# Dividing the softmax weights ahead of their transposes, and multiplying by the values with the values stationary

## The chip, the cores and the metric

The kernel runs on one core of a Trainium2 chip. Its engines work side by side: TensorE (PE in the profile, its weight loads as PEld), VectorE (DVE), ScalarE (ACT), GpSimd (POOL) and SyncE (SP, which issues most of the DMAs). Each engine runs its instructions in a fixed order and waits where an instruction needs something that another engine has not finished. The metric is the time of one execution on the device in microseconds (us): before the change the median of three runs is 1180.84 us (1177.32 to 1181.2).

## What is computed

A small network on 256 tokens with 1024 features, in fp32: a first block with mixers, attention to a memory and a feed forward, and then a second block with two layers. The change is in the attention of these two layers. Each layer has 16 heads of 64 features:

```python
# 4 latent heads ("mla"), 8 dilated heads, 4 heads on selected keys ("dsa"); for each head:
s = q @ k.T * scale
s = where(mask, s, -inf)              # causal; by distance; or causal and among the 64 best keys
p = softmax(s, axis=-1)               # = exp(s - max) / sum
o = p @ v                             # (256 queries, 64 features)
x = x + concat(o of all heads) @ w_o  # then the feed forward
```

## The kernel before

Activations lie feature by feature, 128 features on the partitions and 256 tokens along the row. Weights stream from HBM in chunks; ACT rounds a chunk to `whi` (L409), DVE takes the rest `wlo` (L410), and a product of an activation with a weight is three fp32r matmuls, L428 to L430 (activations are split likewise, by `split`, L457: a copy on ACT, L460, and a difference on DVE, L461). The matmuls of the attention itself are plain fp32 (helper `mm`, L450), and in the trace each of them is two records with a weight load of its own; transposes on PE (helper `tr`, L454) are one record.

The heads go in pairs. The pairs of a layer are called M0 and M1 (latent), D0 to D3 (dilated), S0 and S1 (selected), and the list `ATTN` (L38) sets the order in which their steps are emitted between the projections: M0, M1, D0, D1, D3, D2, S0, S1. The framework's scheduler then orders the instructions of each engine; a projection's three matmuls stand between the steps of the pairs, so that PE has work while a pair's softmax runs.

For a pair, `scores` (L1622) does: the score products of both heads into PSUM, 128 queries by 128 keys and 128 by 256 keys (`pss`, L450); four DVE instructions that add the mask, scale and take the row minimum (L1635, tile `as`); four exponentials on ACT that also give the row sums (L1638, into `ast`); one reciprocal of the four columns of sums (L1640). The weights are not yet divided.

`values` (L1643) does: three transposes a head (`pst<-ident,as`, L454), a copy of each head's 128x384 to SBUF on ACT (`apT`, L1653), then six products with the transposed weights stationary and the values streaming, 64 columns each (`po`, queries on the partitions); one DVE instruction that multiplies by the reciprocals as it reads PSUM (`ao`, L1659); two more transposes (`psf`, L454) back to features on the partitions; and the split into `aoh` and `aol`, which the output projection (`psW`) reads.

Along the same stretch DVE runs the selection of the 64 best keys (`topk`) that S0 and S1 need, and the rotations of queries and keys. POOL has nothing to do there.

Of the kernel before, what the change touches and what calls it, by code (L numbers as in the profile page):

```python
# [16 lines left out]
P = 128  # L17
# [58 lines left out]
def _rot_cols(base, m):  # L76
    """two heads of 64 features, each pair of rotated ones 16 apart"""
    i = np.arange(P)
    return base + 64 * (2 * m + i // 64) + 16 * (i // 32 % 2) + i % 16 + 32 * (i // 16 % 2)
# [276 lines left out]
def weave(*gens):  # L356
    """emits the steps of several mixers in turn"""
    gens = list(gens)
    while gens:
        for g in list(gens):  # L360
            if next(g, gens) is gens:
                gens.remove(g)


class Net:
# [123 lines left out]
    def inv_root(self, pool, v, L, tag):  # L489
        """v: -1/2 of a positive value; L: the value's logarithm; returns the value ** -0.5"""  # L490
        nc = self.nc
        n = v.shape[1]
        y = pool.tile([P, n], F32, tag=tag, name="iy")
        self.xact(y, L, AF.Exp, scale=-0.5)
        t = self.tmp.tile([P, T], F32, tag="irt", name="irt")[:, :n]
        nc.vector.tensor_mul(t, y, y)
        nc.vector.tensor_mul(t, t, v)
        nc.vector.scalar_tensor_tensor(y, t, 1.5, y, ALU.add, ALU.mult)
        return y

    def mean(self, acc, tag):
        """-1/2 (mean + eps) on every partition, and the logarithm of mean + eps"""
# [10 lines left out]
    def cols(self, pool, rB):  # L513
        """[128, 256] the same on every partition -> a column for each token tile"""
# [7 lines left out]
    def sumsq(self, x, gains=(None,), accs=None, join=True, eng=None):  # L522
        """sums over the feature tiles of the squares, one for each gain"""
# [96 lines left out]
    def ffn(self, tag, g, fc, nt):  # L620
# [4 lines left out]
        with self.pool("ffn" + tag) as big, self.pool("fz" + tag, 3) as zp:  # L625
# [13 lines left out]
            # three steps, each two tiles behind the one before, so that no engine waits for another  # L639
# [60 lines left out]
    def block1_mix(self, es):  # L700
# [34 lines left out]
        # rotary tables  # L735
        ang = self.rope_angles(rs)

        # gated delta: q k v with the short convolution
# [111 lines left out]
    def delta(self, s, sm, gates):  # L850
        nc, m, b8, t2 = self.nc, self.mp, self.b8, self.t2
        # beta, log decay
# [17 lines left out]
        # l2 norms  # L870
# [28 lines left out]
        # value rows, scaled by beta  # L899
# [7 lines left out]
        # decay between tokens  # L907
# [20 lines left out]
        for b in range(3):  # L928
            pd = self.pb(512, "psd")
            t = b % 2 if b < 2 else 1  # L930
            # strict and its complement together sum over all tokens
# [23 lines left out]
        # inverse of the unit lower triangle, block doubling  # L955
# [12 lines left out]
        for k in range(1, 7):  # L968
            # only the left half of each pair of blocks changes
# [32 lines left out]
        # solve and read out  # L1002
# [18 lines left out]
    def read_out(self, i, Pm, v):  # L1021
        """Pm: weights [s, block, head, t]; v: [s, tile, head, 64]."""
# [43 lines left out]
    def log_sig(self, f, l):  # L1066
        """l <- ln(1 + exp(-|f|))"""
        nc = self.nc
        nc.scalar.activation(l, f, AF.Abs)
        self.xact(l, l, AF.Exp, scale=-1.0)  # L1070
        self.xact(l, l, AF.Ln, bias=self.one_c)

    def scan_levels(self, nf, lf, qb, k, name):
        """lf: log decay [t, tile, nf*128]; qb: [feat, nf, tile, heads, 128], zero outside its head;
        k: [feat, nf, tile, 128]; returns weights [s, block, head, t]."""
# [62 lines left out]
    def head_rows(self, dst, ps, nh, sc=None):  # L1138
        """dst: [feat, tile, head, 128], zero outside its head's rows; ps: [feat, 256]"""
# [11 lines left out]
    def hgrn(self, xh, xl, gates, tmaj):  # L1151
        nc, m, t2 = self.nc, self.mp, self.t2
        # lower bound
# [85 lines left out]
    def turns(self, xh, xl, cosR, sinR, wait, step):  # L1239
        """queries and keys of the retention, turned; a few products at a time"""  # L1240
# [141 lines left out]
    def block2(self):  # L1382
        from contextlib import ExitStack
        nc, x = self.nc, self.x
        # the first block's last norm and this block's first one
# [21 lines left out]
    def norm_pair(self, pool, s1, s2):  # L1407
        """the root of the first block's last norm, and of it with the next norm"""
# [13 lines left out]
    def attn(self, es, l, xh, xl):  # L1422
# [8 lines left out]
        # latents  # L1431
# [46 lines left out]
        # rotary tables with the norm folded in  # L1478
# [19 lines left out]
        # positions of the keys, scores of the index, queries from the latents  # L1498
# [123 lines left out]
    def scores(self, hs, mask, scale):  # L1622
        """hs: (q, k) of two heads; returns their weights, before the division, and the sums"""
# [16 lines left out]
        nc.vector.reciprocal(st[:, 1], st[:, 0])  # L1640
        return ws, st

    def values(self, ws, st, v, oh, ol, kt):  # L1643
        """v: the values of the two heads; writes feature tile kt of the output."""
        nc, pp = self.nc, self.pp
        po = self.pso.tile([P, 2, 2, 64], F32, tag="o", name="po")
        for i, s in enumerate(ws):
# [3 lines left out]
            # keys 0..127 for all queries, keys 128.. for the later ones  # L1651
            pT = self.p3.tile([P, 384], F32, tag="apT", name="apT")
            nc.scalar.copy(pT, pt)  # L1653
            vi = v[:, :, i * 64:(i + 1) * 64]
            self.mm(po[:, 0, i, :], pT[:, 0:P], vi[:, 0], start=i == 0)
            self.mm(po[:, 1, i, :], pT[:, P:T], vi[:, 0], start=False, stop=False)
            self.mm(po[:, 1, i, :], pT[:, T:384], vi[:, 1], start=False)
        o = pp.tile([P, 2, P], F32, tag="ao", name="ao")
        nc.vector.tensor_mul(o.rearrange("p t (h v) -> p t h v", h=2), po, st[:, 1].unsqueeze(3).to_broadcast([P, 2, 2, 64]))  # L1659
        pf = self.pb(T, "psf")  # L1660
        for t in range(2):
            self.tr(pf[:, t * P:(t + 1) * P], o[:, t])
        self.split(oh[:, kt, :], ol[:, kt, :], pf)
# [19 lines left out]
```

## Time and profile before

| | us |
|---|---|
| median of three runs (lowest, highest) | 1180.84 (1177.32, 1181.2) |
| span of the profiled execution | 1175.3 |
| lowest run less this span | 2.0 |
| median less this span | 5.5 |
| PE busy, share of the span | 1146.0 (98%) |
| DVE, ACT, POOL busy | 937.6 (80%), 668.4 (57%), 110.3 (9%) |
| chain that ended last: PE, DVE, ACT | 87%, 9%, 2% |

The span runs from the first to the last instruction on the core; a run's time has some microseconds around it. A busy PE is not a PE at its peak: matmuls are pipelined, and a record lasts longer than the distance to the next one. So costs on PE are read below from the starts of neighbouring records. The attention of the first of the two layers lies at about 562 to 640 us of the span, that of the second at about 887 to 966 us. The granted clock is full in nearly all slices.

### The profile page before, as it was taken

How to read it: one execution, taken by the hardware profiler on the slowest of the kernel's cores; microseconds unless marked ns; L12 is line 12 of the kernel's file. 1: busy time of each engine (PE TensorE's matmuls, PEld its weight loads, DVE VectorE, ACT ScalarE, POOL GpSimd, SP SyncE). 2: the span in 40 equal slices, each digit the busy share in tenths (PEclk: the TensorE clock that was granted, in tenths of full speed). 3: DMA queues.
4: the chain of work that ended last, by engine and by line, in shares of the span. 5: the costliest groups of instructions: out<-in, count | busy, mean ns of one | idle time of the engine just before them, and what ended most of it. 6: DMA issues, size and time to landing. Idle time of an engine off the chain costs nothing.

```text
span 1175.3 us, 23197 instructions
## 1 busy us (share of the span) xinstructions
PE 1146.0 (98%) x9148; PEld 1103.1 (94%) x9148; DVE 937.6 (80%) x1887; ACT 668.4 (57%) x1178; POOL 110.3 (9%) x137
## 2 busy tenths in 40 slices
PE   7999999999999999998999999999999999999996
PEld 7899888989999999997989999999988999999996
DVE  7987869587599997568897999985578978999854
ACT  6653545466576666554555766664545556766642
POOL 5500201010010000222000200001120002000000
PEclk9999999999999999998999999999999999999998
DMA  6522142556455656544324565555543235565652
GB/s 243 169 73 90 57 146 78 174 180 208 143 167 194 193 186 182 191 151 139 127 93 130 171 200 189 188 184 189 170 146 122 91 126 179 182 195 182 193 183 83
DMA packets 51948, 184.68 MB, mean 157 GB/s; under 512 B 5888, under 2 KB 6784, under 8 KB 51584
## 3 DMA queue, kind: packets, MB, share of 16 engines
q1 hardware_dynamic: 51408, 182.23, 47.9%
q8 instruction: 71, 1.16, 0.4%
q0 software_dynamic: 144, 0.46, 0.2%
q10 hardware_dynamic: 288, 0.52, 0.1%
q14 instruction: 37, 0.30, 0.1%
HBM read 182.14 MB, written 1.05 MB: 156 GB/s over the span
## 4 chain that ended last, share of the span: by engine, by line
PE 87%; DVE 9%; ACT 2%; issue 1%; DMA 1%; SPq 0%; POOL 0%; DVEq 0%; ACTq 0%
PE psU L430 10%; PE psU L429 10%; PE psU L428 10%; PE psD L430 5%; PE psD L428 5%; PE psD L429 5%; PE psp L428 3%; PE po L450 3%; PE psp L429 3%; PE psp L430 3%; PE psW L428 3%; PE psW L430 2%; PE psW L429 2%; DVE wlo L410 2%; PE pss L450 2%; PE pst L441 2%
## 5 line engine op out<-in xcount | busy, mean ns | idle before, releaser
L409 ACT ACTIVATE whi<-raw 128x1024 fp32r<-128x1024 f32 (+5 forms) x411 | 362.8, 898 | 316.6 <-PE psU L429 56.4
L410 DVE TENSOR_TENSOR wlo<-raw,whi 128x1024 fp32r<-128x1024 f32 (+5 forms) x411 | 423.3, 1041 | 140.7 <-ACT whi L409 139.5
L428 PE MATMUL psU<-xh,whi 128*128 128x256 f32 x1056 | 295.4, 280 | 0.0
L430 PE MATMUL psU<-xh,wlo 128*128 128x256 f32 x1056 | 294.9, 279 | 0.2 <-DVE wlo L410 0.2
L429 PE MATMUL psU<-xl,whi 128*128 128x256 f32 x1056 | 294.8, 279 | 0.0
L430 PEld LDWEIGHTS psU<-xh,wlo 128*128 128x128 f32 x1056 | 198.4, 188 | 0.4 <-DVE wlo L410 0.4
L429 PEld LDWEIGHTS psU<-xl,whi 128*128 128x128 f32 x1056 | 198.5, 188 | 0.1
L428 PEld LDWEIGHTS psU<-xh,whi 128*128 128x128 f32 x1056 | 198.5, 188 | 0.1
L428 PE MATMUL psD<-gh,whi 128*128 128x256 f32 x528 | 149.4, 283 | 0.0
L429 PE MATMUL psD<-gl,whi 128*128 128x256 f32 x528 | 149.4, 283 | 0.0
L430 PE MATMUL psD<-gh,wlo 128*128 128x256 f32 x528 | 149.4, 283 | 0.0
L533 POOL TENSOR_TENSOR ssa<-ssa,ssq 128x256 f32<-128x256 f32 x61 | 56.5, 931 | 722.7 <-ACT ssq L531 445.8
L664 DVE SCALAR_TENSOR_TENSOR y<-zb,prm,y 128x256 f32<-128x256 f32 x264 | 114.0, 478 | 0.0
L430 PEld LDWEIGHTS psD<-gh,wlo 128*128 128x128 f32 x528 | 101.4, 192 | 0.0
L429 PEld LDWEIGHTS psD<-gl,whi 128*128 128x128 f32 x528 | 101.3, 192 | 0.0
L428 PEld LDWEIGHTS psD<-gh,whi 128*128 128x128 f32 x528 | 101.3, 192 | 0.0
L428 PE MATMUL psp<-xh,whi 128*128 128x256 f32 (+1 forms) x288 | 85.3, 296 | 0.0
L429 PE MATMUL psp<-xl,whi 128*128 128x256 f32 (+1 forms) x288 | 84.0, 292 | 0.0
L430 PE MATMUL psp<-xh,wlo 128*128 128x256 f32 (+1 forms) x288 | 83.8, 291 | 0.0
L655 ACT ACTIVATE y<-zb,prm 128x256 f32<-128x256 f32 x132 | 67.2, 558 | 5.3 <-DVE zb L651 5.3
L428 PEld LDWEIGHTS psp<-xh,whi 128*128 128x128 f32 (+1 forms) x288 | 55.6, 193 | 3.1 <-issue 2.3
L429 PEld LDWEIGHTS psp<-xl,whi 128*128 128x128 f32 (+1 forms) x288 | 55.3, 192 | 1.1 <-issue 1.0
(456 smaller groups left out, 2342.6 us busy)
## 6 DMA issues: line engine op xcount, KB each, us to landing
raw<-in_wst_dram SPq DMA_DIRECT2D x319, 512.0 KB, 3.5
raw<-in_wst_dram SPq DMA_DIRECT2D x5, 448.0 KB, 3.3
cst<-in_c_dram SPq DMA_DIRECT2D x1, 1664.0 KB, 6.9
raw<-in_wst_dram SPq DMA_DIRECT2D x3, 396.0 KB, 3.3
mem<-in_memT_dram SPq DMA_DIRECT2D x1, 1024.0 KB, 6.1
raw<-in_wst_dram SPq DMA_DIRECT2D x2, 480.0 KB, 3.3
raw<-in_wst_dram SPq DMA_DIRECT2D x2, 420.0 KB, 7.3
raw<-in_wst_dram SPq DMA_DIRECT2D x2, 384.0 KB, 4.1
```

The costliest lines, as they stand in the source:

```text
L409: nc.scalar.activation(hi[:, a:b], raw[:, a:b], AF.Copy)
L410: nc.vector.tensor_sub(lo[:, a:b], raw[:, a:b], hi[:, a:b].bitcast(F32))
L428: nc.tensor.matmul(ps, wh, xh[:, k, :], start=s, stop=False, skip_group_check=True)
L429: nc.tensor.matmul(ps, wh, xl[:, k, :], start=False, stop=False, skip_group_check=True)
L430: nc.tensor.matmul(ps, wl, xh[:, k, :], start=False, stop=e, skip_group_check=True)
L441: nc.tensor.matmul(pss[t], xh[:, k, a], wl, start=False, stop=i == n - 1, skip_group_check=True)
L450: self.nc.tensor.matmul(out, lhsT, rhs, start=start, stop=stop, skip_group_check=True)
L533: (eng or nc.gpsimd).tensor_add(acc, acc, sq)
L655: nc.scalar.activation(y[:, e, u, :], z[:, e, 2:], AF.Identity, scale=fc[:, c + 2:c + 3], **kw)
L664: nc.vector.scalar_tensor_tensor(y[:, e, u, :], zs[u][:, e, j:j + T], fc[:, c + j:c + j + 1], y[:, e, u, :], ALU.mult, ALU.add)
```

## The change

- `scores` ends with four new instructions on POOL that multiply the weights `as` of each head by their reciprocals, in place: 128x128 and 128x256 for each of the two heads.
- `values` transposes the divided weights. The values are now the stationary operand, 64 columns of them, and the transposed weights stream: for each head a product of 256 columns (keys 0 to 127, all queries) and one of 128 columns (keys 128 to 255, later queries). The first head's result goes to partitions 0 to 63 of a bank and the second's to 64 to 127, so `po` has features on the partitions. The multiplication `ao` and the two transposes `psf` are gone; the split reads `po`.
- `apT` has four buffers instead of three.
- Comments and docstrings are emptied; no line number moves by it except within `scores` and `values`.

```diff
@@ scores @@
         nc.vector.reciprocal(st[:, 1], st[:, 0])
+        for i, s in enumerate(ws):
+            for t in range(2):
+                nc.gpsimd.tensor_scalar(s[:, sl[t]], s[:, sl[t]], st[:, 1, t, i:i + 1], None, ALU.mult)
         return ws, st
@@ values @@
-        nc, pp = self.nc, self.pp
-        po = self.pso.tile([P, 2, 2, 64], F32, tag="o", name="po")
+        nc = self.nc
+        po = self.pso.tile([P, 512], F32, tag="o", name="po")[:, :T]
+        pts = []
         for i, s in enumerate(ws):
             pt = self.pb(384, "pst")
             for b in range(3):
                 self.tr(pt[:, b * P:(b + 1) * P], s[:, b * P:(b + 1) * P])
-            pT = self.p3.tile([P, 384], F32, tag="apT", name="apT")
+            pT = self.p3.tile([P, 384], F32, tag="apT", name="apT", bufs=4)
             nc.scalar.copy(pT, pt)
-            vi = v[:, :, i * 64:(i + 1) * 64]
-            self.mm(po[:, 0, i, :], pT[:, 0:P], vi[:, 0], start=i == 0)
-            self.mm(po[:, 1, i, :], pT[:, P:T], vi[:, 0], start=False, stop=False)
-            self.mm(po[:, 1, i, :], pT[:, T:384], vi[:, 1], start=False)
-        o = pp.tile([P, 2, P], F32, tag="ao", name="ao")
-        nc.vector.tensor_mul(o.rearrange("p t (h v) -> p t h v", h=2), po, st[:, 1].unsqueeze(3).to_broadcast([P, 2, 2, 64]))
-        pf = self.pb(T, "psf")
-        for t in range(2):
-            self.tr(pf[:, t * P:(t + 1) * P], o[:, t])
-        self.split(oh[:, kt, :], ol[:, kt, :], pf)
+            pts.append(pT)
+        for i in range(2):
+            r = slice(64 * i, 64 * i + 64)
+            self.mm(po[r], v[:, 0, r], pts[i][:, 0:T], stop=False)
+            self.mm(po[r, P:T], v[:, 1, r], pts[i][:, T:384], start=False)
+        self.split(oh[:, kt, :], ol[:, kt, :], po)
```

The scheduler places the new instructions, and with them the transposes move. PE in the first layer around pair D3, before: the scores of D3 (`pss_7242`, `pss_7251`) follow on the transposes `psf` of D1, and the first transpose of D3 (`pst_7266`) stands behind six projection matmuls.

```order
L454 MATMUL psf_7228<-ident_291,ao_7226 128x128 x2
L450 MATMUL pss_7242<-rk_7109,rq_7108 128x128
L450 MATMUL pss_7242<-rk_7109,rq_7108 128x256
L450 MATMUL pss_7251<-rk_7109,rq_7108 128x128
L450 MATMUL pss_7251<-rk_7109,rq_7108 128x256
L428 MATMUL psp_7361<-xh_6031,whi_7164 128x256
L429 MATMUL psp_7361<-xl_6032,whi_7164 128x256
L430 MATMUL psp_7361<-xh_6031,wlo_7165 128x256
L428 MATMUL psp_7441<-xh_6031,whi_7164 128x256
L429 MATMUL psp_7441<-xl_6032,whi_7164 128x256
L430 MATMUL psp_7441<-xh_6031,wlo_7165 128x256
L454 MATMUL pst_7266<-ident_291,as_7245 128x128
```

The same place on PE now: the four products of D1 (`po_7202`) stand between the first score product of D3 (`pss_7230`) and its other three, right behind D1's transposes (`pst_7203`, `pst_7209`).

```order
L454 MATMUL pst_7203<-ident_291,as_7182 128x128 x3
L454 MATMUL pst_7209<-ident_291,as_7191 128x128 x3
L450 MATMUL pss_7230<-rk_7100,rq_7099 128x128
L450 MATMUL po_7202<-apT_7207,vL_6359 64x256
L450 MATMUL po_7202<-apT_7207,vL_6359 64x128
L450 MATMUL po_7202<-apT_7213,vL_6359 64x256
L450 MATMUL po_7202<-apT_7213,vL_6359 64x128
L450 MATMUL pss_7230<-rk_7100,rq_7099 128x256
L450 MATMUL pss_7239<-rk_7100,rq_7099 128x128
L450 MATMUL pss_7239<-rk_7100,rq_7099 128x256
```

Thirty projection matmuls follow, and one more stands inside the transposes of D3. In the other pairs of the two layers that number is 57 and 57 (M0), 43 and 38 (M1), 22 and 23 (D0), 43 and 37 (D1), 30 and 23 (D3), 24 and 23 (D2), and 20 and 20 behind the scores of S1 (for S0's transposes; S1's follow them with 5 more between).

DVE at the same place, before and now. Before, the multiplication `ao` of D1, a weight chunk's `wlo` and D1's `aol` (`psf` is its source) stand ahead of the mask instructions (ISA) of D3:

```order
L1659 TENSOR_TENSOR ao_7226<-po_7207,ast_7187 128x256
L410 TENSOR_TENSOR wlo_7344<-raw_7341,whi_7343 128x1024
L461 TENSOR_TENSOR aol_6361<-psf_7228,aoh_6360 128x256
L1635 ISA as_7245,anb_7246<-pss_7242,cst2_3728 128x128
L1635 ISA anb_7246 128x1
L1635 ISA as_7245,anb_7246<-pss_7242,cst2_3728 128x256
```

Now `ao` is gone, and `aol` of D1, with `po` as its source, still stands ahead of D3's mask; the reciprocal of D3 follows behind two steps of the selection, as before:

```order
L410 TENSOR_TENSOR wlo_7333<-raw_7330,whi_7332 128x1024
L461 TENSOR_TENSOR aol_6361<-po_7202,aoh_6360 128x256
L1635 ISA as_7233,anb_7234<-pss_7230,cst2_3728 128x128
L1635 ISA anb_7234 128x1
L1635 ISA as_7233,anb_7234<-pss_7230,cst2_3728 128x256
L1635 ISA anb_7234 128x1
L1635 ISA as_7242,anb_7243<-pss_7239,cst2_3728 128x128
L1635 ISA anb_7243 128x1
L1635 ISA as_7242,anb_7243<-pss_7239,cst2_3728 128x256
L1635 ISA anb_7243 128x1
```

The products of a pair have moved ahead to where the next pair's scores are, and the transposes of a pair back behind more projection matmuls.

## Rows read from the trace of the kernel before

**Rows 1.** The page's part 1: busy time, share of the span, instructions.

```profile
PE 1146.0 (98%) x9148; PEld 1103.1 (94%) x9148; DVE 937.6 (80%) x1887; ACT 668.4 (57%) x1178; POOL 110.3 (9%) x137
```

**Rows 2.** Windows, one stretch of the first layer's attention: busy time (instructions) by engine.

```profile
core 0: us, PE busy (x) PEld busy (x) DVE busy (x) ACT busy (x) POOL busy (x), PEclk, DMA share, GB/s
605.00:625.00 20.00, 19.99 (x168) 18.20 (x166) 19.42 (x78) 10.45 (x30) 0.00 (x0) 1.00 0.23 78
```

**Rows 3.** Timeline of pair M0, first layer: start, duration, engine, line, operation.

```profile
569.66 0.17 DVE L1640 RECIPROCAL ast<-ast 128x4 f32<-128x4 f32 x1
569.75 0.82 PE L454 MATMUL pst<-ident,as 128*128 128x128 f32 x6
570.27 0.86 ACT L1653 COPY apT<-pst 128x384 f32<-128x384 f32 x2
570.80 1.55 PE L450 MATMUL po<-vA,apT 128*128 128x64 f32 x12
575.06 0.44 PE L454 MATMUL psf<-ident,ao 128*128 128x128 f32 x2 [0.19 <-DVE ao L1659]
```

**Rows 4.** Timeline, PE: scores of M1 (128 rows) and of D0 (64 rows).

```profile
575.33 1.48 PE L450 MATMUL pss<-ka,qa 128*128 128x128 f32 x8
583.04 0.93 PE L450 MATMUL pss<-rk,rq 64*128 64x128 f32 x8
```

**Rows 5.** Timeline, PE: first and last of seven products of a projection.

```profile
587.50 0.28 PE L428 MATMUL psp<-xh,whi 128*128 128x256 f32 x1
588.21 0.28 PE L428 MATMUL psp<-xh,whi 128*128 128x256 f32 x1
```

**Rows 6.** Groups by form, POOL: out<-in, count, busy us and mean ns.

```profile
L803 POOL TENSOR_SCALAR rs<-rs,cst 128x256 f32<-128x256 f32 x1 | 0.9, 931 | 0.3 <-DMA cst<-in_c_dram 0.3
L806 POOL TENSOR_SCALAR rs<-rs 128x256 f32<-128x256 f32 x7 | 6.2, 891 | 0.6
L824 POOL TENSOR_SCALAR rs<-rs 128x256 f32<-128x256 f32 x1 | 0.5, 495 | 0.1
```

**Rows 7.** Timeline, DVE: pair D3 of the first layer, mask to reciprocal.

```profile
609.33 0.29 DVE L1635 CUSTOM_DVE_ANT_0 as<-pss,cst 128x128 f32<-128x128 f32 x1
611.62 0.17 DVE L1640 RECIPROCAL ast<-ast 128x4 f32<-128x4 f32 x1
```

**Rows 8.** Instructions of the split's two lines: min/median/max ns.

```profile
L460 ACT ACTIVATE aoh<-psf x16: 363/384/386, 575.5 to 965.1; 128x256 fp32r<-128x256 f32 x16
L461 DVE TENSOR_TENSOR aol<-psf,aoh x16: 416/419/425, 576.4 to 965.6; 128x256 fp32r<-128x256 f32 x16
```

**Rows 9.** Timeline: reciprocal of S0 and transposes of S1; second layer's M0.

```profile
632.53 0.17 DVE L1640 RECIPROCAL ast<-ast 128x4 f32<-128x4 f32 x1
636.19 0.82 PE L454 MATMUL pst<-ident,as 128*128 128x128 f32 x6
894.19 0.18 DVE L1640 RECIPROCAL ast<-ast 128x4 f32<-128x4 f32 x1
896.24 0.82 PE L454 MATMUL pst<-ident,as 128*128 128x128 f32 x6
```

**Rows 10.** Timeline, POOL and DVE at one time.

```profile
535.96 2.74 POOL L1511 TENSOR_TENSOR ka<-rz,kp 32x512 f32<-32x512 f32 x2 [0.57 <-DVE irt L497]
537.50 1.21 DVE L1495 SCALAR_TENSOR_TENSOR mq<-iy,rT 128x2 f32<-128x2 f32 x1
538.64 0.14 DVE L1496 TENSOR_TENSOR mk<-iy,rT 128x2 f32<-128x2 f32 x1
```

**Rows 11.** Windows, PE: busy time, then the granted clock, DMA share, GB/s.

```profile
882.60:886.02 3.42, 2.39 (x22) 1.00 0.48 156
886.02:889.43 3.41, 3.41 (x15) 0.50 0.50 159
589.33:592.75 3.42, 2.91 (x26) 1.00 0.48 153
```

## The prediction

> **What bounds the kernel now.** I read the page's engine totals first, then windows over the attention, then the timeline of single pairs. PE is busy for 98% of the span [rows 1], so a change counts by what it takes off PE's stream or by the time for which it makes PE wait. In the attention the margin is thinner still: in the stretch where the selection runs, PE is busy for 19.99 of 20 us and DVE for 19.42, while POOL has nothing [rows 2]. PE does not wait there for the softmax because the scheduler has put just enough projection matmuls between a pair's scores and its transposes. So two questions decide: what PE is spared, and whether the projection matmuls that now stand between still cover the longer way from scores to transposes.
>
> **What PE is spared.** Before, a pair's products take 1.55 us on PE and its two transposes back 0.44 us [rows 3]. The four new products stream 256 and 128 columns for each head, in eight records. The trace has the same eight halves twice as score products: 1.48 us where each uses the whole array, 0.93 us where the two heads use different halves of the array's rows, because then the heads run side by side [rows 4]. Whether two halves of its columns do so too, no row of before shows, so 0.93 and 1.48 us are the two ends. I take 1.41: side by side, but the second head starts one copy later, 0.48 us (the two copies in 0.86 us follow each other on ACT [rows 3], and 0.48 is my reading of the later one's length within them). That spares 1.55 + 0.44 - 1.41 = 0.58 us a pair, 9.3 us for 16 pairs (1.06 and 0.51 at the two ends: 17 and 8 us). Against it, in D0, D3 and D2 of each layer the products cut the scores of the next pair in two; the cut takes the first score product out of its parallel run. The price lies between nothing and the 0.55 us by which side by side is faster [rows 4]; 0.4 us for 6 places is 2.4 us. PE is spared 6.9 us. The Trainium skill's page "TensorEngine Tiling (Array Packing)", section Key Properties, says that different tiles of the array work in parallel and that a change of the tiling mode drains it. The trace agrees for halves of the rows only; by the page the products would take 0.93 us, and the sum would be some 7 us lower where PE, and not the wait below, is the limit.
>
> DVE loses 16 `ao` instructions. I count that as nothing: the shorter DVE queue helps only where the wait for DVE ends last, and in the chain below POOL comes behind it. The fourth buffer of `apT` releases no wait that the rows show: nothing.
>
> **What the division costs.** The divisor is there after the reciprocal; then come four POOL instructions. The nearest row has the very form, one operation with a column as the scalar: 0.93 us for 128x256 (L803 in [rows 6]); with a constant as the scalar seven of them average 0.89 us (L806). One with two operations took 0.49 us (L824), which I keep as the lower end. For 128x128 no row stands; half, 0.47 us, is an estimate, its ends 0.25 (half of 0.49) and 0.93. With gaps of 0.1 between them the four take 2 x (0.93 + 0.47) + 0.3 = 3.1 us; the lower end is 1.8 us, the upper one above 3.7 us.
>
> Before, the first head's transposes needed only its exponentials; now the transposes of a pair's last slice need the reciprocal of both heads and all four POOL instructions. And because DVE's `aol` of a pair stands ahead of the mask of the next, and is now fed by the late products, pairs that follow one another form a ring. From the end of one pair's transposes to the end of the next one's:
>
> - the second copy is there 0.72 us after the stream of transposes has ended (569.75 + 0.66 to 570.27 + 0.86 [rows 3], 0.66 being six at 0.11, an estimate from the 0.82 us of the row less the last one's tail);
> - products 0.93, `aoh` 0.38, `aol` 0.42 [rows 4, 8];
> - from the first mask instruction to the end of the reciprocal 611.79 - 609.33 = 2.46 us [rows 7];
> - POOL 3.1, and two transposes behind its last instruction 0.3.
>
> That is 8.3 us. PE's own work in that ring: first score product 0.2 and the products, which end 1.65 us after the transposes (0.72 + 0.93); three score products 0.75 (0.93 less a quarter, rounded up); n projection matmuls at (588.21 - 587.50) / 6 = 0.118 us [rows 5]; transposes with the change of kind 0.76. That is 3.16 + 0.118 n. D3 of the first layer has n = 31, so 6.8 us, and PE waits 1.5 us. Likewise D0 with 23: 2.4 us; D2 with 25: 2.2 us. In the second layer n is 24, 24 and 23: 2.3, 2.3 and 2.4 us. M1 has n = 44 and 39 and whole-array scores (0.5 more), and a weight chunk with a shuffle ahead of its reciprocal on DVE, about 0.7 us more in the ring: 0.2 and 0.7 us. D1 has about 120 projection matmuls and eight index products since D0's transposes, some 19 us of PE: nothing, but it would be up to 2.5 us if the selection on DVE holds its mask back as far as it does before.
>
> The pairs at the ends. M0 of the first layer: PE came to its transposes at 569.75, and the reciprocal ended at 569.83; its chain up to there has not changed, so the last slice comes 3.1 + 0.3 us later and PE, which was through 0.6 us after 569.75, waits 2.8 us. In the second layer the reciprocal ended at 894.37 and the transposes started at 896.24 [rows 9]: 0.9 us. S0 and S1: S0's reciprocal ended at 632.70; two pairs' POOL work (6.2 us) and 0.3 us lead to 639.2 us, where S1's transposes were through at 636.8 [rows 9]: 2.4 us, and the same for the second layer.
>
> Sum of the waits: first layer 2.8 + 0.2 + 2.4 + 0 + 1.5 + 2.2 + 2.4 = 11.5 us; second 0.9 + 0.7 + 2.3 + 0 + 2.3 + 2.4 + 2.4 = 11.0 us; together 22.5 us. With POOL at 1.8 us the ring is 7.0 us and the same lists give about 7 us.
>
> **The clock.** After a stretch of 3.42 us with PE busy for 2.39 us the granted clock was at the lower level, 1.2 GHz, for 3.41 us; after one with 2.91 us it stayed at 2.4 GHz [rows 11]. A wait of 2.4 us is longer than the idle time in the first. At half clock 3.4 us do 1.7 us less work. Behind the waits of M1 and D3 the ring hides that; behind D0 and D2, where long runs of projections follow, it does not. Four places, half of them taken: 3.4 us. The ends are none and 6.8 us.
>
> **Sum.** 1175.3 - 6.9 + 22.5 + 3.4 = 1194.3 us of span. The median stands 5.5 us above the profiled span, so 1199.8, say 1200 us.
>
> **Rivals.**
>
> *POOL is quick (chance 0.25).* If these instructions run at L824's 0.49 us or faster, the waits shrink to 7 us or less and no drop of the clock comes: 1175.3 - 6.9 + 7 = 1175.4 of span, 1180.9 us; at half that time again the waits fall to about 1 us, and the time is 1169.4 + 5.5 = 1175 us. For it: L824, and an idle POOL. Against it: ten of ten one-operation rows on 256 columns would have to mislead, eight of which stand in rows 6. The Trainium skill's "GPSIMD Engine Reference", section Engine selection, says that elementwise work with one input runs there at about line rate; its 1.03 cycles an element (section 3.1) would be an estimated 0.22 us. L803 and L806 are four times that, so the trace does not bear it out. This case ends at 1175 to 1181 us, faster or not to be told from before.
>
> *The two engines get in each other's way (0.15).* While POOL ran `ka` for 2.74 us, a DVE instruction on 128x2 elements took 1.21 us, and the next small one, alone, 0.14 us [rows 10]. If each pair's POOL work has to let one weight chunk of 1.2 us on DVE go first, the ring is 9.5 us, and some 12 waits grow by 1.2: 1214 us. For it: DVE is busy for 97% of that stretch. Against it: DVE, too, stands still when PE does, so its queue is shorter by then. The skill's page "SBUF — State Buffer", section on rules for kernel authors, says the later of the two is blocked while DVE has two SBUF inputs and POOL reads SBUF; the rows agree.
>
> *The halves do not run side by side (0.15).* The change then does not do what its layout is for: 1.48 us instead of 0.93 in each ring, 0.55 us more in 12 places: 1206 us. For it: no row shows column halves at once. Against it: row halves do.
>
> The forecast itself has 0.45. The range for 8 times in 10 is 1177 to 1217 us: below it lies the quickest part of the first rival, at its top the second rival with a few drops of the clock more. A measurement of this kernel tells 0.3%, 3.5 us, from no change, that is 1177.3 to 1184.4 us. The first rival's 0.25 divides into 0.13 faster and 0.12 the same; all else is slower, 0.75.
>
> **What would show it.** In the new profile: POOL instructions of line 1643 at about 0.93 and 0.47 us; PE idle ahead of `pst` with POOL as the releaser, some 2 us in D0 and D2 and about 20 us in all; a distance of about 8 us between the transposes of D1, D3 and D2, where it was 6 to 7; the eight records of `po` in 0.9 or 1.5 us; slices of the attention with a lower granted clock behind D0 and D2. The prediction is wrong if POOL's releases cost PE less than 8 us in all, or if the four instructions together stay below 2 us.

## The result, and the profile after

The changed kernel takes 1234.78 us (median of four runs, 1232.5 to 1236.31), before it was 1179.08 us in the same series; the ratio is 1.0472, 95% interval 1.0451 to 1.0493. The forecast was slower, but 1200 us, and its range ended at 1217 us: the direction was right, the size was three times too small. The profiled span is 1232.7 us, 57.4 us more than before (the medians differ by 55.7 us; the profiled run of before was one of the quick ones).

The page's part 1 and the line of granted clocks of its part 2 (40 slices of the span, tenths of full speed), after the change:

```profile
PE 1170.5 (95%) x9052; PEld 1105.5 (90%) x9052; DVE 934.8 (76%) x1871; ACT 671.1 (54%) x1178; POOL 170.7 (14%) x201
...
PEclk9999999999999999979888999999998889999999
```

Against [rows 1], PE is busy for 24.5 us more, though it has 96 instructions fewer: it did the same work at a lower clock. The slices with an 8 lie at 585 to 678 and 924 to 1017 us, in the two attentions; the 7 is at 524 to 555 us, ahead of them. POOL has 60 us more. The windows show it by stage (busy time and number of instructions of each engine, then the mean granted clock), first before, from the first score product of a layer to its last product with the values:

```profile
core 0: us, PE busy (x) PEld busy (x) DVE busy (x) ACT busy (x) POOL busy (x), PEclk, DMA share, GB/s
561.70:638.81 77.11, 76.21 (x623) 70.36 (x622) 68.98 (x240) 42.20 (x109) 0.00 (x0) 1.00 0.34 112
887.03:964.13 77.10, 76.97 (x617) 71.06 (x617) 67.39 (x237) 42.33 (x108) 0.00 (x0) 0.98 0.32 104
```

The same two stretches after, in the same columns:

```profile
565.84:672.71 106.87, 89.23 (x577) 72.18 (x575) 67.75 (x233) 43.70 (x109) 30.33 (x32) 0.87 0.25 84
918.76:1021.62 102.86, 85.98 (x571) 69.76 (x569) 66.56 (x231) 42.82 (x108) 30.71 (x32) 0.88 0.25 82
```

Their lengths grow by 29.8 and 25.8 us, 55.6 of the 57.4. PE stands still for 106.87 - 89.23 = 17.6 and 16.9 us, where it was 0.9 and 0.1. And in the stretches at the lower clock, 1.2 GHz (called drops below), 27.3 and 23.9 us long, PE is busy for 26.8 and 22.3 us; at half the clock about half of that is lost (six score records take 1.64 us in a drop and 0.93 outside, both shown further on). The account of the span:

| | before | after | difference | forecast |
|---|---|---|---|---|
| PE idle in the two attentions | 1.0 | 34.5 | +33.5 | +22.5 |
| lost to 1.2 GHz there (half of PE's busy time at it) | 1.2 | 24.5 | +23.3 | +3.4 |
| PE's busy time, counted at 2.4 GHz, whole span | 1138.3 | 1136.9 | -1.4 | -6.9 |
| outside the attentions: idle and clock | | | +2.0 | 0 |
| sum | | | +57.4 | +19.0 |

The line outside the attentions is mostly no work of the change: a stretch at the lower clock around 540 us, ahead of the first changed instruction, lasts 6.8 us in some profiles and 13.7 us in others, here in the longer form, and as long in the fastest version below.

Who waited for POOL's line 1643, from the view of that line (minimum, median, maximum in ns; then us and times):

```profile
L1643 POOL TENSOR_SCALAR as<-as,ast x64: 596/918/1925, 574.1 to 1017.4; 128x128 f32<-128x128 f32 x32, 128x256 f32<-128x256 f32 x32
...
who waited for it (us, times):
  PEld pst L454: 43.8, 52
  PE pst L454: 32.4, 45
```

The timeline of POOL, three pairs of the first layer with four instructions each, and then single instructions, the last two side by side on POOL and DVE:

```profile
623.79 2.98 POOL L1643 TENSOR_SCALAR as<-as,ast 128x128 f32<-128x128 f32 x4 [21.63 <-DVE ast L1640]
633.30 3.50 POOL L1643 TENSOR_SCALAR as<-as,ast 128x128 f32<-128x128 f32 x4 [6.53 <-DVE ast L1640]
643.28 4.09 POOL L1643 TENSOR_SCALAR as<-as,ast 128x128 f32<-128x128 f32 x4 [6.47 <-DVE ast L1640]
```

```profile
623.79 0.60 POOL L1643 TENSOR_SCALAR as<-as,ast 128x128 f32<-128x128 f32 x1 [21.63 <-DVE ast L1640]
...
625.85 0.93 POOL L1643 TENSOR_SCALAR as<-as,ast 128x256 f32<-128x256 f32 x1
...
645.05 1.42 POOL L1643 TENSOR_SCALAR as<-as,ast 128x128 f32<-128x128 f32 x1
...
644.79 1.21 DVE L410 TENSOR_TENSOR wlo<-raw,whi 128x1024 fp32r<-128x1024 f32 x1
```

0.60 and 0.93 us stand for the forecast's 0.47 and 0.93, answering [rows 6]. But a 128x128 piece that meets a weight chunk's `wlo` takes 1.42 us: it is through 0.47 us after DVE is. Of the 32 small pieces 13 meet a chunk and take 1.11 to 1.67 us, the other 19 take 0.60 to 0.87. So the four take 2.97 us at the least and 3.8 in the mean (61.0 us of POOL in the two attentions for 16 pairs).

The ring from D1's transposes to D3's, in the timeline of all engines:

```profile
626.83 0.44 PE L454 MATMUL pst<-ident,as 128*128 128x128 f32 x2 [0.57 <-POOL as L1643]
...
627.30 0.48 ACT L1657 COPY apT<-pst 128x384 f32<-128x384 f32 x1 [1.00 <-PE pst L454]
...
627.76 1.61 PE L450 MATMUL po<-apT,vL 128*64 128x256 f32 x8
...
629.31 1.64 PE L450 MATMUL pss<-rk,rq 64*128 64x256 f32 x6
...
629.83 0.42 DVE L461 TENSOR_TENSOR aol<-po,aoh 128x256 fp32r<-128x256 f32 x1 [2.35 <-ACT aoh L460]
...
630.67 0.29 DVE L1635 CUSTOM_DVE_ANT_0 as<-pss,cst 128x128 f32<-128x128 f32 x1 [0.42 <-PE pss L450]
...
632.97 0.17 DVE L1640 RECIPROCAL ast<-ast 128x4 f32<-128x4 f32 x1
...
633.30 3.50 POOL L1643 TENSOR_SCALAR as<-as,ast 128x128 f32<-128x128 f32 x4 [6.53 <-DVE ast L1640]
...
636.86 0.44 PE L454 MATMUL pst<-ident,as 128*128 128x128 f32 x2 [0.57 <-POOL as L1643]
```

From 627.27 (626.83 + 0.44) to 637.30 us are 10.03 us, for which the forecast had 8.3, and the next ring is 10.6. Its steps: second copy to 627.78; products until 629.37, 1.61 us against 0.93 forecast, with the lower clock on; `aoh` and `aol` to 630.25; then 0.42 us in which DVE waits for score products, which the `po` products had cut and which run at the lower clock too; mask to reciprocal 2.47 us (forecast 2.46); POOL from 633.30 to 636.80; transposes. The clock in the same stretch, by windows of PE:

```profile
core 0: us, PE busy (x), PEclk, DMA share, GB/s
623.98:627.39 3.41, 1.66 (x7) 1.00 0.00 0
627.39:630.80 3.41, 3.41 (x16) 0.50 0.48 154
634.22:637.63 3.41, 2.18 (x13) 1.00 0.34 85
637.63:641.04 3.41, 3.41 (x16) 0.50 0.18 73
```

After a stretch with 1.66 of 3.41 us busy the clock is at half for the next 3.41 us, and after one with 2.18 too, as [rows 11] had it. In the two attentions there are 15 such stretches, three times two in a row. They stand behind every pair but M0 and D3 of the second layer, with S0 and S1 counted as one place.

### The profile page after: what moved, and what is told of

Read it like the earlier page. It is cut to its first block, busy times and chain, and to the rows that moved or that the text cites. A ratio compares the mean times of both kernels' runs of the same rounds, so it can differ in the third digit from the quotient of the medians.

```text
span 1232.7 us, 23107 instructions
## 1 busy us (share of the span) xinstructions
PE 1170.5 (95%) x9052; PEld 1105.5 (90%) x9052; DVE 934.8 (76%) x1871; ACT 671.1 (54%) x1178; POOL 170.7 (14%) x201
## 4 chain that ended last, share of the span: by engine, by line
PE 80%; DVE 9%; issue 5%; POOL 4%; ACT 2%; DMA 0%; SPq 0%; DVEq 0%; POOLq 0%
PE psU L430 10%; PE psU L428 10%; PE psU L429 10%; PE psD L430 5%; PE psD L429 5%; PE psD L428 5%; POOL as L1643 4%; PE po L450 3%; PE psW L428 2%; PE psW L430 2%; PE psW L429 2%; PE pss L450 2%; PE psp L428 2%; PE psp L429 2%; PE psp L430 2%
## 5 line engine op out<-in xcount | busy, mean ns | idle before, releaser
L1643 POOL TENSOR_SCALAR as<-as,ast 128x128 f32<-128x128 f32 x64 | 61.0, 969 | 193.0 <-DVE ast L1640 153.6
```

What stands on the lines that cost most here:

```text
L1643: nc.gpsimd.tensor_scalar(s[:, sl[t]], s[:, sl[t]], st[:, 1, t, i:i + 1], None, ALU.mult)
```

## The experiments

Two theories stood after the result. A: the wait of the transposes for POOL and the drops of the clock that follow make the loss. B: the products on column halves, which cut score products and change the array's shape, make it. C and D put it on POOL and DVE in each other's way: C says that this alone is the loss, D that any POOL work there costs, however short. A1 and A2 part A: the clock falls because PE stands still, or for another reason. E, for the versions without POOL, says that DVE's full queue sets the wait. All runs in one table. The ratio is to runs of the kernel before in the same series (medians 1177.2 to 1179.1 us); idle time and time at 1.2 GHz, in us, are those of the two attentions in the profile of each, and PE's work is its busy time counted at 2.4 GHz over the span:

| kernel | us | ratio to before (95%) | PE idle | at 1.2 GHz | PE's work |
|---|---|---|---|---|---|
| before | 1179 | 1 | 1.0 | 2.4 | 1138 |
| the change | 1234.8 | 1.0472 (1.0451 to 1.0493) | 34.5 | 51.2 | 1137 |
| no_division | 1180.9 | 1.0017 (1.0001 to 1.0033) | 1.5 | 2.9 | 1139 |
| old_products_pool | 1262.5 | 1.0723 (1.0698 to 1.0747) | 36.0 | 91.3 | 1142 |
| act_division | 1183.6 | 1.0047 (1.0028 to 1.0065) | 1.5 | 3.3 | 1141 |
| dve_division | 1179.4 | 1.0018 (1.0001 to 1.0035) | 6.6 | 0 | 1136 |
| half_division | 1191.0 | 1.0099 (1.0076 to 1.0122) | 13.2 | 5.2 | 1134 |
| fill_between | 1234.2 | 1.0472 (1.0453 to 1.0492) | 25.0 | 17.0 | 1161 |
| fill_wait | 1232.8 | 1.0446 (1.0422 to 1.0470) | 8.5 | 3.4 | 1183 |
| late_division | 1184.9 | 1.0065 (1.0042 to 1.0087) | 2.8 | 2.6 | 1141 |
| lag_pool | 1199.3 | 1.0181 (1.0157 to 1.0205) | 18.9 | 13.7 | 1137 |
| lag_dve | 1179.8 | 1.0015 (0.9996 to 1.0033) | 6.1 | 0 | 1139 |
| lag_mix | 1179.7 | 0.9997 (0.9981 to 1.0013) | 5.3 | 3.4 | 1132 |
| mix | 1176.2 | 0.9972 (0.9955 to 0.9990) | 4.5 | 0 | 1134 |

**Which half of the change.** no_division leaves out POOL's instructions:

```diff
-        for i, s in enumerate(ws):
-            for t in range(2):
-                nc.gpsimd.tensor_scalar(s[:, sl[t]], s[:, sl[t]], st[:, 1, t, i:i + 1], None, ALU.mult)
```

> The changed kernel without the four POOL instructions of a pair; the weights stay undivided, so the division is left out. Theory A (the wait for POOL and the clock drops behind it make the loss): PE idle in the two attentions falls from 34.5 us to under 4 us, no stretch at the lower clock follows a pair, and the time is 1165 to 1177 us (before 1179, less up to 0.9 us a pair by the shorter products and the two missing transposes). Rival B (the products on column halves, their change of array shape and the cut score products make the loss): more than half of the 56 us stays, the time is above 1207 us.

old_products_pool adds the same lines to the kernel before.

> The kernel before with the four POOL divisions of a pair added ahead of the transposes; its products and its multiplication by the reciprocals stay, so it divides twice. Theory A: the whole loss comes with the POOL instructions, 1225 to 1245 us, with 30 us or more of PE idle and 40 us or more at the lower clock in the two attentions. Rival B: the loss is in the products, which are the old ones here, so under 1200 us.

The windows over the two attentions of no_division (columns as above):

```profile
566.16:644.49 78.33, 77.57 (x582) 66.15 (x580) 67.19 (x234) 43.50 (x110) 0.00 (x0) 1.00 0.34 109
891.72:970.62 78.90, 78.17 (x575) 66.65 (x574) 65.81 (x231) 42.69 (x108) 0.00 (x0) 0.98 0.31 101
```

and of old_products_pool:

```profile
563.73:681.59 117.86, 98.96 (x632) 87.93 (x631) 71.08 (x241) 44.68 (x110) 31.14 (x32) 0.81 0.25 79
930.15:1049.83 119.68, 102.61 (x625) 90.19 (x625) 70.33 (x238) 43.35 (x108) 31.18 (x32) 0.80 0.22 71
```

Without the division 54 us of the 56 are gone, with it alone the loss is larger still: B falls. Yet both expectations were missed on one side. no_division gains nothing by its products: PE's work is 1139 us (the reason is in the next section). And old_products_pool is 28 us slower than the whole change. PE is idle there as long (36 us), but at 1.2 GHz for 91 us instead of 51. What its pairs have more than those of the change is the old way behind the transposes, twelve product records, `ao` and two transposes. That this length is what costs the extra drops is the likely reading; no run takes it apart.

**Another engine for the division.** act_division and dve_division put it on ACT and on DVE:

```diff
-                nc.gpsimd.tensor_scalar(s[:, sl[t]], s[:, sl[t]], st[:, 1, t, i:i + 1], None, ALU.mult)
+                nc.scalar.activation(s[:, sl[t]], s[:, sl[t]], AF.Identity, scale=st[:, 1, t, i:i + 1])
```

> The changed kernel with the division on ACT in place of POOL, the same four instructions. An ACT copy of 128x384 takes 0.48 us in the trace and an exponential of 128x256 about 0.5; four instructions are estimated at 1.6 us against POOL's 3.8. Theory A: PE waits less by up to 2.2 us a pair, idle below 12 us, few stretches at the lower clock, 1180 to 1200 us. Rival B: like the changed kernel, above 1215 us. Rival C (POOL and DVE hold each other up, and that alone is the loss): all of it goes, 1165 to 1178 us.

```diff
+                nc.vector.tensor_scalar(s[:, sl[t]], s[:, sl[t]], st[:, 1, t, i:i + 1], None, ALU.mult)
```

> The changed kernel with the division on DVE in place of POOL. A DVE instruction over 128x256 takes 0.42 us with two inputs in this trace, so the four are at most 1.4 us, and they stand in DVE's own queue behind the reciprocal, where weight chunks of 1.2 us can get between. Theory A: 1175 to 1200 us, about as with ACT. Rival B: above 1215 us. Rival C: 1165 to 1178 us.

The line's group in dve_division (minimum, median, maximum in ns), and its window over 600 to 640 us:

```profile
L1643 DVE TENSOR_SCALAR as<-as,ast x64: 266/314/351, 573.7 to 967.3; 128x128 f32<-128x128 f32 x32, 128x256 f32<-128x256 f32 x32
```

```profile
600.00:640.00 40.00, 38.30 (x295) 33.07 (x294) 38.77 (x156) 21.74 (x58) 0.00 (x0) 1.00 0.28 88
```

Both came out in A's ranges and above C's, dve_division by little more than 1 us. They do not tell A from C, though: no_division takes 1180.9 us, so by C too they could not end much lower. On DVE an instruction takes 0.27 to 0.35 us, a pair 1.23 us instead of 3.8, and no drop of the clock is left in the attentions. DVE is busy for 38.8 of 40 us there.

**How much of POOL.** half_division divides only the first 128 columns of each head:

```diff
-            for t in range(2):
+            for t in range(1):
                 nc.gpsimd.tensor_scalar(s[:, sl[t]], s[:, sl[t]], st[:, 1, t, i:i + 1], None, ALU.mult)
```

> The changed kernel with POOL dividing only the 128x128 part of each head (0.60 us without DVE beside it); the 128x256 part stays undivided, so half of the division is left out. POOL then takes about 1.3 us a pair instead of 3.8, some 2.5 us less. Theory A (PE waits for POOL, and drops of the clock follow the waits): the wait of about 2.1 us a pair goes almost wholly, and with it the drops: 1180 to 1195 us. Rival D (any POOL work ahead of the transposes costs, through the port that it shares with DVE, and not through its length): above 1205 us.

1191 us, inside A's range. The first 1.5 us of POOL a pair (24.35 us of POOL in the two attentions) cost 10 us against no_division, the other 2.3 us cost 44. In idle time a microsecond of POOL costs about the same in both parts, half a microsecond (11.7 us for 24.4, 21.3 for 36.7); the difference is the clock, of whose 51.2 us at the lower level only 5.2 are there in half_division. D falls.

**Is it the standing still that lowers the clock?** fill_between gives PE work that nothing needs:

```diff
             pt = self.pb(384, "pst")
+            if i == 1:
+                for _ in range(12):
+                    self.tr(pt[:, 0:P], ws[0][:, 0:P])
```

> The changed kernel with twelve more transposes of the first head's weights on PE ahead of the second head's transposes; their results are overwritten, so the result stays. They are 16 x 12 x 0.11 = 21 us of PE work, placed where PE waits for POOL's second half. Theory A1 (the clock falls because PE stands still, and it costs about 23 us in the two attentions): nearly no half-clock stretch behind a pair, and as the fillers lie in the waits they cost little: 1205 to 1222 us. Rival A2 (the clock falls for another reason, as POOL's and DVE's load): the half-clock stretches stay, and the time is 1235 to 1256 us.

The time lay outside both ranges, 1 us below A2's, as the work filled only the second half of POOL's chain, and the scheduler took projection matmuls away for it: 25 us of idle time stayed. The clock moved with the idle time, 17 us at 1.2 GHz instead of 51. fill_wait fills both halves:

```diff
             pt = self.pb(384, "pst")
+            for _ in range(14 if i == 0 else 12):
+                if i == 0:
+                    self.tr(pt[0:8, 0:P], st.rearrange("p a b c -> p (a b c)"))
+                else:
+                    self.tr(pt[:, 0:P], ws[0][:, 0:P])
```

> The changed kernel with PE kept at work through the whole wait: fourteen transposes of the reciprocals' tile ahead of the first head's transposes and twelve of the first head's weights ahead of the second's, all overwritten afterwards, so the result stays. They are 16 x 26 x 0.11 = 46 us of PE work. Theory A1 (the clock falls only because PE stands still): idle time in the two attentions under 10 us of 34.5, half-clock stretches there under 7 us of 51, so 1235 + 46 - 25 - 24 = 1222 to 1240 us in spite of the work added. Rival A2 (the clock falls for another reason, or wakes no higher): 30 us or more at the lower clock stay there, and the time is above 1250 us.

Its windows over the two attentions, and PE's timeline between two pairs:

```profile
565.55:661.56 96.01, 92.42 (x732) 78.76 (x730) 65.87 (x231) 41.95 (x107) 26.01 (x32) 1.00 0.25 83
917.02:1014.11 97.09, 92.20 (x715) 77.98 (x713) 65.30 (x229) 40.92 (x106) 30.43 (x32) 0.98 0.24 76
```

```profile
628.47 1.69 PE L454 MATMUL pst<-ident,ast 128*8 128x128 f32 x14 [0.33 <-DVE ast L1640]
630.00 2.26 PE L454 MATMUL pst<-ident,as 128*128 128x128 f32 x18
632.18 1.50 PE L450 MATMUL po<-apT,vL 128*64 128x256 f32 x8
633.62 0.93 PE L450 MATMUL pss<-rk,rq 64*128 64x128 f32 x8
```

PE goes straight from the 14 useless transposes that wait for the reciprocal into the 18 that wait for POOL (12 of them useless), and the clock is full all through the first layer; 3.4 us at 1.2 GHz are left, at the start of the second. With 46 us more of work the kernel is as fast as the change. A1 is shown: POOL works nearly as long as in the change (56 us against 61), and the clock stays up when PE has something to do.

**The distance from scores to transposes.** lag_pool puts a pair's values behind the next pair's scores, with the division on POOL:

```diff
-        "uq3", "uk1", "l0", "Mv0", "M1", "Mv1", "D0", "Dv0", "l1", "l2", "side", "l3", "side", "D1", "Dv1", "side",
-        "side", "D3", "side", "Dv3", "side", "D2", "side", "side", "s0", "sides", "Dv2", "s1", "S0", "S1", "Sv0",
+        "uq3", "uk1", "l0", "M1", "Mv0", "D0", "Mv1", "l1", "Dv0", "l2", "side", "l3", "side", "D1", "side",
+        "side", "D3", "Dv1", "side", "side", "D2", "Dv3", "side", "side", "s0", "sides", "Dv2", "s1", "S0", "S1", "Sv0",
```

> The changed kernel, POOL division included, with the steps in another order: the values of a pair come behind the scores of the next pair, for M0 to D3. So between a pair's scores and its transposes lie another pair's scores and, by the order of instructions, 25 to 45 projection matmuls and the transposes of the pair before. Theory A: POOL's chain of 3.8 us is covered where pairs overlap; half or more of the idle 34.5 us goes, and the drops with it: 1185 to 1212 us. Rival D (POOL's work itself slows DVE, whatever it is covered by): above 1220 us.

```profile
561.96:652.03 90.07, 80.09 (x577) 66.81 (x575) 67.05 (x233) 42.98 (x109) 28.06 (x32) 0.94 0.31 100
898.09:984.12 86.03, 77.09 (x571) 64.76 (x569) 66.55 (x231) 42.27 (x108) 27.67 (x32) 0.98 0.30 98
```

These two windows, again the two attentions, have 18.9 us of idle time. The order of steps alone gives back about 35 us of the 56, with nearly the same POOL work (55.7 us). C falls as the whole cause: the same POOL instructions are there and most of the loss is gone. In the change, what DVE's instructions add to POOL's is an estimated 13.5 us (61.0 less 16 times 2.97), against a loss of 56; what these 13.5 us cost by themselves no run shows.

**Versions that might beat both.** late_division leaves POOL's instructions out, carries the reciprocals to the features' partitions and divides behind the products (the lines at `...` make two tiles):

```diff
-        self.split(oh[:, kt, :], ol[:, kt, :], po)
+        pf = self.pb(T, "psf")
+        for i in range(2):
+            r = slice(64 * i, 64 * i + 64)
+            for t in range(2):
+                self.mm(pf[r, t * P:(t + 1) * P], st[:, 1, t, i:i + 1].to_broadcast([P, 64]), self.ident[:, 0:P], start=t == 0)
+        ...
+        nc.scalar.copy(rp, pf)
+        nc.vector.tensor_mul(o, po, rp)
+        self.split(oh[:, kt, :], ol[:, kt, :], o)
```

> The new products, but the division behind them: four small products of the reciprocals (as a stationary of 64 equal columns) with the identity bring each head's reciprocals to its 64 partitions, ACT copies them to SBUF, and one DVE instruction multiplies the products by them. Nothing waits for the reciprocal ahead of the transposes. Theory A: no waits, so about as the kernel before; PE spares some 0.2 to 0.5 us a pair in the products and pays 0.44 to 0.88 us for the small ones instead of 0.31: 1172 to 1184 us. Rival B (the products on column halves are dear in themselves): above 1190 us.

1184.9 us, a little above A's range: PE's work is 3 us above that of before. lag_dve is lag_pool's order with the division on DVE:

> The order of steps with the values of a pair behind the scores of the next, and the division on DVE (1.23 us a pair). With the old order this division left 6.6 us of PE idle in the two attentions and 1179 us, for PE work 2.6 us below the kernel before. Theory A: the overlap takes the idle time to about 1 to 3 us, so 1172 to 1177 us, the first version below the kernel before. Rival E (DVE is at its limit there, 38.8 of 40 us, and its queue, not the distance of scores and transposes, sets the wait): no gain, 1177 to 1185 us.

It came out in rival E's range. mix divides the first head on ACT and the second on DVE, in the order of the change, lag_mix the same in lag_pool's order:

```diff
+                if i == 0:
+                    nc.scalar.activation(s[:, sl[t]], s[:, sl[t]], AF.Identity, scale=st[:, 1, t, i:i + 1])
+                else:
+                    nc.vector.tensor_scalar(s[:, sl[t]], s[:, sl[t]], st[:, 1, t, i:i + 1], None, ALU.mult)
```

> The first head divided on ACT, the second on DVE, in the changed kernel's order of steps. About 1 us from the reciprocal to the last divided weight instead of POOL's 3.8. Theory A: idle 2 to 6 us, no drops of the clock, 1174 to 1182 us. Rival E (DVE at its limit): below the division on DVE alone (1179) by 3 us or more.

> As the version with the division on DVE and the values behind the next pair's scores, but ACT divides the first head and DVE the second, so DVE has 0.6 us a pair less to do. Theory A: like that version, 1172 to 1178 us. Rival E (DVE at its limit): 3 us or more below it.

mix, over its two attentions:

```profile
565.67:644.93 79.26, 77.35 (x603) 67.87 (x601) 71.77 (x250) 50.49 (x127) 0.00 (x0) 1.00 0.34 115
887.85:966.78 78.93, 76.33 (x597) 66.89 (x595) 70.48 (x248) 49.18 (x126) 0.00 (x0) 1.00 0.32 109
```

mix is 0.3% faster than before (1 to 4.5 per thousand), the lowest of the versions tried and the only one whose interval lies below 1; a difference of that size is about the least that these runs can tell. Its interval also lies below that of dve_division, whose DVE has 0.6 us a pair more, but its time fits A's range as well as E's. lag_mix missed both ranges: it should have come out 3 us below lag_dve by E, and came out level with it. So that DVE's queue sets the wait is not shown.

lag_mix has the least PE work and is yet not faster than mix. The record shows where that goes: its profile has 10.2 us at 1.2 GHz between 867 and 894 us, where that of mix has none, and seven of its twelve runs have a mean granted clock of 0.985 or 0.986, but one of mix's ten. At 0.989 the two agree: 1176.1 to 1178.1 us in five runs of mix, 1176.0 to 1177.8 in four of lag_mix (1177.4 to 1179.5 in six of before). Why these drops come more often in lag_mix stays open.

## Why the prediction was wrong

**The term that failed: the clock.** The forecast took "four places, half of them taken: 3.4 us", with 6.8 us as the upper end; it measured 23.3 us, in 15 stretches. The step that failed is "Behind the waits of M1 and D3 the ring hides that". Hidden would be a lower clock whose stretch PE waits through anyway. But PE is busy in it (26.8 of 27.3 us in the first layer): the products and the next scores stand right behind the transposes and lie in the ring themselves. So half of PE's work in each drop is lost, inside the ring as outside. fill_wait shows that the drops go when the idle time goes. That M0, D1 and the S pairs would drop as well was not counted at all. A drop does not lengthen the waits in sum: old_products_pool has 91.3 us at 1.2 GHz and 36.0 us idle, the change 51.2 and 34.5.

**The waits: right in kind, a third too small.** PE is idle for 33.5 us more, against 22.5. By places, the idle time in both layers together, the 1.0 us of before included:

| | forecast | measured |
|---|---|---|
| D0, D3 and D2 | 13.1 | 11.9 |
| M1 | 0.9 | 4.8 |
| D1 | 0 | 6.9 |
| M0, S0 and S1 | 8.5 | 11.0 |

The ring itself takes 10.0 and 10.6 us instead of 8.3, by three things that the rows show: POOL's four take 3.5 to 4.1 us beside DVE's weight chunks, not 3.1; products 1.61 us instead of 0.93 at the lower clock; 0.42 us more for the cut scores. Yet its waits are no longer than forecast, as PE's own work in it is slower too. What was put too low are M1 and D1 (1.1 of D1's 6.9 us are another wait, for ACT). For D1 the forecast had "nothing", with up to 2.5 us if the selection on DVE holds its mask back; that happened, here in the first layer:

```profile
617.11 0.93 PE L450 MATMUL pss<-rk,rq 64*128 64x128 f32 x8
...
620.38 0.29 DVE L1635 CUSTOM_DVE_ANT_0 as<-pss,cst 128x128 f32<-128x128 f32 x1
...
623.45 0.18 DVE L1640 RECIPROCAL ast<-ast 128x4 f32<-128x4 f32 x1
...
624.45 0.33 PE L454 MATMUL pst<-ident,as 128*128 128x128 f32 x1 [1.19 <-POOL as L1643]
```

The scores end at 618.04, the mask starts 2.34 us later, and PE is at the transposes before the reciprocal is there. In M1 of the first layer a weight chunk stands ahead of the exponentials on ACT and waits for PE:

```profile
584.82 1.06 ACT L409 ACTIVATE whi<-raw 128x1024 fp32r<-128x1024 f32 x1 [3.77 <-PE psp L429]
```

The two engines in each other's way are the second rival, at 0.8 us a pair instead of 1.2. It had 0.15 as a case by itself, but it belonged into the forecast's sum. The Trainium skill, page "SBUF — State Buffer", summary of rules for kernel authors, says that while DVE has two SBUF inputs and POOL reads SBUF, the second to issue waits until the first is done. For POOL behind DVE the trace agrees: eleven of the thirteen small pieces that meet a `wlo` end 0.47 us after it. For DVE behind POOL it mostly does not: the fifteen `wlo` that start inside one of these instructions take 1.21 to 1.48 us, where 1.22 is usual.

**POOL's price: right.** 0.60 and 0.92 us stand for 0.47 and 0.93; the rival of a quick POOL had nothing for it. The Trainium skill's page "GPSIMD Engine Reference", section Engine selection, says that one-input work runs at about line rate; that does not hold for this form: 0.92 us for 256 columns, where DVE takes 0.35.

**The halves: they run side by side where both heads are there.** The last products of S1, at full clock:

```profile
671.83 0.88 PE L450 MATMUL po<-apT,vS 128*64 128x256 f32 x8
```

0.88 us for eight records, beside the 0.93 of halves of the rows and 1.48 of the whole array in [rows 4]; the rival that they can't falls. The Trainium skill, page "TensorEngine Tiling (Array Packing)", Key Properties, says that different tiles of the array can work in parallel, and this trace agrees. Where one head's copy comes late, they follow each other: eight records take 1.50 us in fill_wait's line above, and 1.50 to 1.56 in all its pairs.

**What PE is spared: less, and it goes with the order on PE.** In the change it is 1.4 us instead of 6.9. Only four of its sixteen pairs have their products at full clock (0.88 to 1.28 us), so its 1.4 us is not taken apart here. The other versions show what it goes with. In mix the products of the sixteen pairs take 1.0 us a pair in the mean, and PE's work is 4.7 us below that of before; in no_division they take 1.4, and the work is 0.9 us above. There projections break the transposes up more (55 runs of transposes against 32), so that the second head comes later. So both ends that the forecast gave, 0.93 and 1.48 us, occur in about that size.

The cut of the next pair's scores was put at 0.4 us. The second layer's D3, where the clock of the change is full, agrees:

```profile
986.89 0.48 PE L450 MATMUL pss<-rk,rq 64*128 64x128 f32 x2
987.31 1.09 PE L450 MATMUL po<-apT,vL 128*64 128x256 f32 x8
988.33 0.93 PE L450 MATMUL pss<-rk,rq 64*128 64x256 f32 x6
```

The first two score records hold PE for 0.42 us, and the other six still take 0.93, as long as all eight when they are whole. In mix the products stand in the middle, between the two heads' scores, and each half runs alone:

```profile
618.02 0.92 PE L450 MATMUL pss<-rk,rq 64*128 64x128 f32 x4
618.87 1.03 PE L450 MATMUL po<-apT,vL 128*64 128x256 f32 x8
619.83 0.92 PE L450 MATMUL pss<-rk,rq 64*128 64x128 f32 x4
```

## What to carry to other kernels

Where PE sets the time, a step that is put on the way from scores to transposes costs what it takes beyond the cover, and then the lower clock of what stands behind the wait: here 33.5 and 23.3 us. A drop costs half of PE's work in it wherever PE is busy then, inside a ring of dependent pairs too. So the waits are summed first, pair by pair, also those of a pair whose softmax another engine's queue holds back; and if they come pair after pair, every one is given its drop, half of the work behind it lost. Move such a step to the engines with the shortest instruction for it, and share it between two; here that turned 4.7% slower into 0.3% faster, which is hardly more than the time of before.

## What was not expected of the hardware

A POOL instruction of 0.60 us took up to 1.67 us beside one of DVE. And useless matmuls, 46 us of them by estimate, cost nothing while they kept PE from standing still: 1232.8 us with them, 1234.8 without.
